# Three of four feed-forwards in a planned engine order, with seven-product pairs 5 to 21 and their sums in three PSUM banks

## The chip, the core and the metric

The kernel runs on one core of a Trainium2 chip. A core has a matrix engine (TensorE, PE in the profile), a vector engine (VectorE, DVE), an activation engine (ScalarE, ACT), a general engine (GpSimd, POOL) and one that issues transfers (SyncE, SP). Matrix products land in PSUM, which has eight banks of 128 partitions by 512 f32 values. All other tiles lie in SBUF. Each engine runs its own instructions strictly in order, and waits at an instruction until the semaphores it names are set. The metric is the device time of one execution in microseconds (us).

## The reference, cut to what matters

```python
D_MODEL, SEQ, D_FF, DEPTH = 1024, 512, 2816, 2

def swiglu_ffn(x, w_gate, w_up, w_down):
    return (jax.nn.silu(x @ w_gate) * (x @ w_up)) @ w_down

for layer in range(DEPTH):
    h = h + 0.5 * swiglu_ffn(rms_norm(h, ffn1_norm[layer]), ffn1 weights[layer])
    # layer 0: Conformer convolution module; layer 1: stick-breaking attention on shared K and V
    h = h + mixer(rms_norm(h, mix_norm[layer]))
    h = h + 0.5 * swiglu_ffn(rms_norm(h, ffn2_norm[layer]), ffn2 weights[layer])
    # after layer 0: K and V for layer 1 = rms_norm(h, kv_norm) @ w_kv
return rms_norm(h, final_norm)
```

All values are f32. There are four feed-forwards, numbered 0 to 3 here in the order of execution. Numbers 1 and 2 follow each other without a mixer between them (the end of layer 0 and the start of layer 1).

## The kernel before, in words

**Tiles.** Activations lie with features on partitions and the 512 tokens along the free axis, in eight chunks of 128 features. Every f32 operand of a product is split into a high part (a cast to fp32r, on ScalarE, line L249) and a low part (the difference, on VectorE, L250), and a product is three matmuls: high by high, high by low, low by high (`mm3`, L397 to L399). A weight unit is 128 x 1024 f32 (512 KB). It is loaded by SyncE into one of three `raw` buffers and split into one of three `whi` and one of three `wlo` buffers (`fetch`, L364 to L387). `unit` (L389) hands out the oldest unit and loads the next one.

**A feed-forward** (`ffn`, L490 to L640) works in three thirds, hidden columns 0 to 7, 8 to 15 and 16 to 21 of 128 each. In a third, each hidden column f takes a gate unit and an up unit, its *pair*. Then eight down products `pd` (L397 to L399) add the third to the residual `xpar` (L631). A **plain pair** is 2 units x 8 chunks x 3 = 48 matmuls with 512 columns. A **seven-product pair** (`seven`, L532 to L576) computes the same two products as a 2 x 2 block product by the Strassen-Winograd scheme: seven block products of 4 x 3 matmuls with 256 columns, 84 in all. Its weight sums are made by `sevens` (L327 to L362) from the two raw units: `st` holds two sums (L344, L346), L345 and one more subtraction make two others in place in `raw`, and all are split like weights (`sh`/`sl`, `uh`/`ul`, second unit `whi`/`wlo`). These buffers exist once each. The matching sums of the activations are made once per feed-forward by `right_sums` (L501 to L519). The list `SEVEN` names the columns that are computed so: 11, 10 and 11 of the 22 in feed-forwards 1, 2 and 3, mixed with plain pairs. Feed-forward 0 has none.

**The sums of the seven products.** A seven-product pair takes three PSUM banks `pg`. ScalarE copies the first product (`m1`, L560) and the third (`m5`, L564) out, VectorE makes `v6` (L562) and `v7` (L566) and adds the rest in L568 to L576.

**Norm.** Each feed-forward's input is normalised by a factor per token. `Norm.chunk` (L457 to L478) takes each residual chunk when it is final: ScalarE writes `xhi_f` (L463) and its square `sq_f` (L476), VectorE writes `xlo_f` (L464) and adds the square to `acc_f` (L477). When all eight are in, `factor` (L480) sums `acc_f` over features with four small matmuls (`token_sums`, L425 to L430), takes the root, and spreads it to `rb`, which multiplies the gate and up products where they leave PSUM (L571, L572, L576; L611 in plain pairs).

**Order.** The program is written feed-forward by feed-forward as above, and the framework's scheduler orders the instructions of each engine across these statements, by its own estimate of when each is ready. PSUM banks of a feed-forward rotate through one tag with seven buffers.

The program's three feed-forwards with seven-product pairs run, in the profiled execution, from about 553 to 905 us (number 1), 905 to 1260 us (number 2) and 1537 to 1885 us (number 3).

Of the kernel before, what the change touches and what calls it, by code (L numbers as in the profile page):

```python
# [198 lines left out]
def decoder_kernel(ctx, tc, xin, gu, dna, dnb, pw1, pw2, kq, wv, wo, out):  # L199
# [126 lines left out]

    def sevens(i, src):  # L327

        p = beside_hidden[0]
        raw = [wp.tile([P, UNIT], F32, name=f"raw{i}_{o}", tag="raw", bufs=3) for o in range(2)]
        hi, lo = (
            [wp.tile([P, UNIT], F32R, name=f"{n}{i}_0", tag=n, bufs=3),
             p.tile([P, UNIT], F32R, name=f"{n}{i}_1", tag=n, bufs=1)]
            for n in ("whi", "wlo")
        )
        for o in range(2):
            nc.sync.dma_start(raw[o], src[o])
        st = p.tile([P, UNIT], F32, name=f"st{i}", tag="st", bufs=STS)  # L340
        a11, a12, a21, a22 = (quarter(raw[o], e) for o in range(2) for e in range(2))
        s1, s2 = (quarter(st, e) for e in range(2))
        split(hi[0], lo[0], raw[0])
        V.tensor_add(s1, a21, a22)  # L344
        V.tensor_sub(a21, a11, a21)  # L345
        V.tensor_sub(s2, s1, a11)  # L346
        sh, sl = (p.tile([P, UNIT], F32R, name=f"s{n}{i}", tag=f"s{n}", bufs=1) for n in "hl")
        split(sh, sl, st)
        split(hi[1], lo[1], raw[1])
        V.tensor_sub(a12, a12, s2)  # L350
        uh, ul = (p.tile([P, NC // 2, P], F32R, name=f"u{n}{i}", tag=f"u{n}", bufs=1) for n in "hl")
        split(uh, ul, a12)

        def part(h, l, e):
            return lambda q: (quarter(h, e)[:, q, :], quarter(l, e)[:, q, :])

        return {
            "11": part(hi[0], lo[0], 0), "12": part(hi[0], lo[0], 1),
            "s3": part(hi[1], lo[1], 0), "22": part(hi[1], lo[1], 1),
            "s1": part(sh, sl, 0), "s2": part(sh, sl, 1),  # L360
            "s4": lambda q: (uh[:, q, :], ul[:, q, :]),
        }  # L362
# [127 lines left out]
    def ffn(idx, norm, done, early=None, beside=None, sums=None, late=None, tail=None):  # L490
        with ExitStack() as c:
# [6 lines left out]
            halves = [slice(0, T // 2), slice(T // 2, T)]
            right = []

            def right_sums(q):  # L501


                x = []
                for k in (2 * q, 2 * q + 1):
                    f = tp.tile([P, T], F32, name=f"xs{idx}_{k}", tag="sq", bufs=2)
                    V.tensor_add(f, *(y.bitcast(F32) for y in norm.x[k]))
                    x.append(f)
                b11, b12, b21, b22 = (y[:, h] for y in x for h in halves)
                t = hp.tile([P, 2 * T], F32, name=f"ts{idx}_{q}", tag="st", bufs=STS)  # L510
                t1, t2, t3, t4 = (t[:, j * T // 2 : (j + 1) * T // 2] for j in range(4))
                V.tensor_sub(t1, b12, b11)
                V.tensor_sub(t2, b22, t1)
                V.tensor_sub(t3, b22, b12)
                V.tensor_sub(t4, b21, t2)
                tiles = [sums_at(q, o) for o in range(2)]
                for o, (h, l) in enumerate(tiles):
                    split(h, l, t[:, o * T : (o + 1) * T])
                right.append(tiles)  # L519

            def sums_at(q, o):
                if sums is not None:
                    return [
                        sums[0].tile([P, T], F32R, name=f"t{n}{idx}_{q}_{o}", tag=sums[1] + n, bufs=NC)
                        for n in ("hi", "lo")
                    ]
                return [
                    hp.tile([P, T], F32R, name=f"t{n}{idx}_{q}_{o}", tag=f"t{n}", bufs=NC)
                    for n in ("hi", "lo")
                ]  # L530

            def seven(n, tg, tu):  # L532
                w = unit()

                def x(row, h):
                    return lambda q: [y[:, halves[h]] for y in norm.x[2 * q + row]]

                def t(j):
                    return lambda q: [y[:, halves[j % 2]] for y in right[q][j // 2]]


                at_ = [
                    ps.tile([P, T], F32, name=f"pg{n}_{j}", tag="ps", bufs=7)[:, : T // 2]
                    for j in range(3)
                ]
                m1, m5, v6, v7 = (
                    hp.tile([P, T // 2], F32, name=f"{m}_{n}", tag=m, bufs=1)
                    for m in ("m1", "m5", "v6", "v7")
                )

                def product(j, left, rhs, first):
                    for q in range(NC // 2):
                        a, b, d = w[left](q), rhs(q), at_[j]
                        last_ = q == NC // 2 - 1
                        PE.matmul(d, a[0], b[0], start=first and q == 0, stop=False, skip_group_check=True)  # L555
                        PE.matmul(d, a[0], b[1], start=False, stop=False, skip_group_check=True)  # L556
                        PE.matmul(d, a[1], b[0], start=False, stop=last_, skip_group_check=True)  # L557

                product(0, "11", x(0, 0), True)
                A.copy(m1, at_[0])  # L560
                product(1, "s2", t(1), True)
                V.tensor_add(v6, at_[1], m1)  # L562
                product(2, "s1", t(0), True)
                A.copy(m5, at_[2])  # L564
                product(1, "s3", t(2), False)
                V.tensor_add(v7, at_[1], m1)  # L566
                product(2, "s4", x(1, 1), False)
                V.tensor_add(tg[:, halves[1]], at_[2], v6)  # L568
                product(0, "12", x(1, 0), False)
                product(1, "22", t(3), False)  # L570
                V.tensor_mul(tg[:, halves[1]], tg[:, halves[1]], rb[:, halves[1]])  # L571
                V.tensor_mul(tg[:, halves[0]], at_[0], rb[:, halves[0]])  # L572
                last[0] = A.activation(tg, tg, AF.Silu)
                V.tensor_add(tu[:, halves[1]], v7, m5)
                V.tensor_add(tu[:, halves[0]], at_[1], m1)
                V.tensor_mul(tu, tu, rb)  # L576
# [903 lines left out]
```

## Time and profile before

| | |
|---|---|
| median of 3 runs | 1906.84 us (1905.96 to 1907.18) |
| span of the profiled execution | 1904.9 us |
| TensorE busy | 1884.1 us, 99% of the span |
| VectorE busy | 1318.5 us, 69% |
| ScalarE busy | 872.7 us, 46% |
| seven-product pairs | 32 of 66 pairs in feed-forwards 1 to 3 |

In the lines of the profile, `L398 PE MATMUL pg<-xlo_f,whi` is line 398 of the kernel before, on TensorE, writing tile `pg` from `xlo_f` and `whi`. A timeline row begins with the start in us and the duration in us. A bracket at its end tells how long the engine was idle ahead of it and what ended that. The rows of windows give a stretch of the span, its length, and for each engine its busy time with the number of instructions in brackets; then come the granted TensorE clock (1.00 is full speed), the share of time in which DMA engines were busy, and GB/s. The time of a matmul in a record holds its passage through the array, which overlaps the next one, so that the cost of a matmul in a dense stretch is the distance between starts.

### The profile page before, as it was taken

To read this page: it belongs to the slowest core of one execution; us is meant where nothing else is said; L and a number is where in the kernel's file an instruction comes from. 1 tells how busy PE (TensorE), PEld (TensorE's weight loads), DVE (VectorE), ACT (ScalarE), POOL (GpSimd) and SP (SyncE) were. 2 spreads that over 40 slices of the span, in tenths; PEclk is the share of its full clock that TensorE was granted. 3 is DMA by queue.
4 is the path that set the end of the run, shared out by engine and by line. 5 is a ranking of instruction groups with operands and counts; after the bars stand their busy time and mean duration, and the time that the engine had idled before them with its cause. 6 is when DMAs were issued, how large, how long until landed. Compare 5 with 4: busy or idle time off the path is not lost.

```text
span 1904.9 us, 26577 instructions
## 1 busy us (share of the span) xinstructions
PE 1884.1 (99%) x10236; PEld 1630.4 (86%) x10236; DVE 1318.5 (69%) x2139; ACT 872.7 (46%) x1385; POOL 288.1 (15%) x267
## 2 busy tenths in 40 slices
PE   9999999999999999999999999999999999999997
PEld 7888888878998889898888988888888788898896
DVE  6544434589869577576775857778989688676575
ACT  5423424586644234244333423446778644343333
POOL 0212302079700000000000000004554100000001
PEclk9999999999999999999999999999999999999998
DMA  5756746444422323333433232442323133332322
GB/s 203 251 180 232 275 146 216 158 172 144 161 78 89 105 89 117 100 94 96 143 111 100 89 111 89 127 155 83 89 70 93 49 123 100 100 95 95 111 86 70
DMA packets 74254, 237.84 MB, mean 125 GB/s; under 512 B 8464, under 2 KB 11152, under 8 KB 74128
## 3 DMA queue, kind: packets, MB, share of 16 engines
q1 hardware_dynamic: 65776, 209.41, 34.0%
q10 hardware_dynamic: 8352, 26.74, 3.8%
q8 instruction: 80, 1.31, 0.3%
q14 instruction: 46, 0.38, 0.1%
HBM read 200.46 MB, written 31.46 MB: 122 GB/s over the span
## 4 chain that ended last, share of the span: by engine, by line
PE 94%; DVE 2%; POOL 1%; ACT 1%; issue 1%; DMA 0%; POOLq 0%; DVEq 0%; ACTq 0%
PE pg L397 11%; PE pg L398 11%; PE pg L399 11%; PE pd L398 8%; PE pd L397 8%; PE pd L399 8%; PE pg L557 6%; PE pg L556 6%; PE pg L555 6%; PE z L1192 2%; PE pa L397 1%; PE pa L398 1%; PE pa L399 1%; PE pv L397 1%; PE pk L397 1%
## 5 line engine op out<-in xcount | busy, mean ns | idle before, releaser
L249 ACT CAST whi<-raw 128x1024 fp32r<-128x1024 f32 (+2 forms) x310 | 313.2, 1013 | 634.6 <-PE pd L398 226.8
L250 DVE TENSOR_TENSOR wlo<-raw,whi 128x1024 fp32r<-128x1024 f32 (+2 forms) x310 | 367.8, 1191 | 43.1 <-ACT whi L249 42.7
L398 PE MATMUL pg<-xlo_f,whi 128*128 128x512 f32 x896 | 349.7, 391 | 0.0
L397 PE MATMUL pg<-xhi_f,whi 128*128 128x512 f32 x896 | 349.0, 391 | 0.6 <-ACT whi L249 0.6
L399 PE MATMUL pg<-xhi_f,wlo 128*128 128x512 f32 x896 | 349.4, 390 | 0.0
L398 PE MATMUL pd<-hlo,whi 128*128 128x512 f32 x686 | 266.2, 389 | 0.0
L399 PE MATMUL pd<-hhi,wlo 128*128 128x512 f32 x686 | 265.1, 389 | 0.0
L397 PE MATMUL pd<-hhi,whi 128*128 128x512 f32 x686 | 264.1, 389 | 0.0
L397 PEld LDWEIGHTS pg<-xhi_f,whi 128*128 128x128 f32 x896 | 169.0, 189 | 35.2 <-ACT whi L249 1.5
L399 PEld LDWEIGHTS pg<-xhi_f,wlo 128*128 128x128 f32 x896 | 168.6, 188 | 34.7 <-DVE wlo L250 0.3
L398 PEld LDWEIGHTS pg<-xlo_f,whi 128*128 128x128 f32 x896 | 168.8, 188 | 33.6
L631 DVE SCALAR_TENSOR_TENSOR xpar<-pd,xpar 128x512 f32<-128x512 f32 x93 | 63.7, 689 | 170.6 <-PE pd L399 170.6
L399 PEld LDWEIGHTS pd<-hhi,wlo 128*128 128x128 f32 x686 | 128.8, 188 | 26.8
L397 PEld LDWEIGHTS pd<-hhi,whi 128*128 128x128 f32 x686 | 128.8, 188 | 26.7
L398 PEld LDWEIGHTS pd<-hlo,whi 128*128 128x128 f32 x686 | 128.8, 188 | 26.6
L1092 POOL TENSOR_SCALAR_AFFINE_SELECT tri<-ones 128x128 f32<-128x128 f32 x1 | 0.6, 592 | 703.7 <-DVE tu L612 703.7
L250 POOL TENSOR_TENSOR plo<-praw,phi 128x1024 fp32r<-128x1024 f32 x24 | 59.0, 2461 | 275.7 <-ACT phi L249 273.9
L875 POOL TENSOR_TENSOR ws<-ws,pr 128x256 f32<-128x256 f32 (+1 forms) x90 | 91.0, 1023 | 58.2 <-ACT pr L873 54.6
L249 ACT CAST hhi<-tu 128x512 fp32r<-128x512 f32 x88 | 54.3, 621 | 87.9 <-DVE tu L586 49.2
L886 DVE SCALAR_TENSOR_TENSOR pc<-gl,xpar,pc 128x512 f32<-128x512 f32 (+1 forms) x145 | 88.3, 646 | 3.9 <-PE pc L865 2.2
L611 DVE TENSOR_TENSOR tu<-pg,r_f 128x512 f32<-128x512 f32 x56 | 38.6, 689 | 74.2 <-PE pg L399 74.2
L556 PE MATMUL pg<-tlo,whi 128*128 128x256 f32 x256 | 72.5, 283 | 0.0
(359 smaller groups left out, 4195.0 us busy)
## 6 DMA issues: line engine op xcount, KB each, us to landing
raw<-in_gu_dram SPq DMA_DIRECT2D x174, 512.0 KB, 3.5
raw<-in_dna_dram SPq DMA_DIRECT2D x64, 512.0 KB, 3.6
praw<-in_pw_dram SPq DMA_DIRECT2D x24, 512.0 KB, 4.4
aparth<-phi ACTq DMA_DIRECT2D x24, 512.0 KB, 2.7
apartl<-plo ACTq DMA_DIRECT2D x24, 512.0 KB, 3.8
raw<-in_dnb_dram SPq DMA_DIRECT2D x32, 384.0 KB, 3.4
whi<-aparth SPq DMA_DIRECT2D x21, 512.0 KB, 3.3
wlo<-apartl SPq DMA_DIRECT2D x21, 512.0 KB, 4.2
```

What stands on the lines that cost most here:

```text
L249: ins = A.copy(dst_hi, src)
L250: (G if on_pool else V).tensor_sub(dst_lo, src, dst_hi.bitcast(F32))
L397: PE.matmul(ps, w[0], x[0], start=first, stop=False)
L398: PE.matmul(ps, w[0], x[1], start=False, stop=False)
L399: PE.matmul(ps, w[1], x[0], start=False, stop=last)
L555: PE.matmul(d, a[0], b[0], start=first and q == 0, stop=False, skip_group_check=True)
L556: PE.matmul(d, a[0], b[1], start=False, stop=False, skip_group_check=True)
L557: PE.matmul(d, a[1], b[0], start=False, stop=last_, skip_group_check=True)
L611: V.tensor_mul(tu, pt[1], rb)
L631: V.scalar_tensor_tensor(res[d], pd, 0.5, res[d], op0=ALU.mult, op1=ALU.add)
L875: add("G", 1.28 * f + 0.1 * half, lambda pr=pr: G.tensor_add(accp, accp, pr()[:, at0]), r=[pr], w=[at_], rank=rank)
L886: add("V", 0.66 * f + 0.06 * half, lambda x=x, q=q: V.scalar_tensor_tensor(pc(), x(), q, pc(), op0=ALU.mult, op1=ALU.add), r=[gl], w=[pc], ...
```

## The change

Feed-forward 0 stays in `ffn`. Feed-forwards 1, 2 and 3 move to a new function `planned`, which lists every step with its engine, an assumed duration, what it reads and writes, and a rank, in a `Plan`. The plan then picks, again and again, the step that can start earliest by the assumed durations (among equals the lowest rank), and the instructions of TensorE, VectorE and ScalarE are issued exactly in that order, without the framework's scheduler.

```diff
-SEVEN = {1: (5, 6, 8, 9, 11, 12, 14, 16, 17, 19, 20), 2: (6, 8, 10, 11, 13, 14, 16, 17, 19, 20), 3: (5, 6, 8, 9, 11, 12, 14, 16, 17, 19, 20)}
+SEVEN = {i: tuple(range(5, 22)) for i in (1, 2, 3)}
...
-    ffn(1, n_f2, n_f1.chunk, sums=(xp, "x"))
+    planned(1, n_f2, n_f1, sums=(xp, "x"), ahead=2)
...
-        ffn(2, n_f1, n_mix.chunk, early=kv_input, sums=(kvp, ""), late=kv_back)
+        planned(2, n_f1, n_mix, early=kv_input, sums=(kvp, ""), late=kv_back)
...
-    ffn(3, n_f2, n_out.chunk, tail=tail)
+    planned(3, n_f2, n_out, tail=tail, ahead=TAIL)
```

In `planned`, three of the eight PSUM banks are set apart for the sums of seven-product pairs (`u0`, `u1`, `g1`), and five are left to rotate. The sums are no longer added up by VectorE: after a product, ScalarE copies the bank's content to the bank where the next products go on adding.

```diff
+            banks = [ps.tile([P, T], F32, name=f"bank{idx}_{i}", tag="ps", bufs=8) for i in range(8)]
+            seeds = {x: banks[i][:, :N2] for i, x in enumerate(("u0", "u1", "g1"))}
...
+            add("PE", 0.5, lambda: token_sums(ss()[:, :4], norm.acc), w=[ss], rank=-2)
...
+                for x in seeds.values():
+                    PE.matmul(x, onesr, norm.x[0][0][:, :N2], start=True, stop=True)
+            add("PE", 0.4, seed, w=list(seeds), rank=-2)
...
+                product(g0b, g0, w["11"], x(0, 0), [], True, r_)
+                add("A", 0.35, lambda: A.copy(ub, g0b()), r=[g0], w=[u], rank=rank - 1)
+                product(mb, m, w["s1"], t(0), sums_, True, r_)
+                product(lambda: ub, u, w["s2"], t(1), sums_, False, r_)
+                add("A", 0.35, lambda: A.copy(m5(), mb()), r=[m], w=[m5], rank=rank - 0.5)
+                add("A", 0.35, lambda: A.copy(gb, ub), r=[u], w=[g1], rank=rank - 1)
+                product(g0b, g0, w["12"], x(1, 0), [], False, r_)
+                add("V", 0.35, lambda: V.tensor_mul(tg()[:, lo_], g0b(), rb[:, lo_]), r=[g0, "rb"], w=[tg], rank=rank)
+                product(lambda: ub, u, w["s3"], t(2), sums_, False, r_)
+                add("A", 0.35, lambda: A.copy(u3(), ub), r=[u], w=[u3], rank=rank - 1)
...
+                product(lambda: gb, g1, w["s4"], x(1, 1), [], False, r_)
...
+                product(lambda: ub, u, w["22"], t(3), sums_, False, r_)
```

The assumed durations are 3.0 us for a weight transfer, 0.95 and 1.14 for the two halves of a split, 1.44 for a product of twelve matmuls, 0.682 for three matmuls with 512 columns, and 0.15 from the end of a step to the start of one that waits for it. Weights of a seven-product pair are loaded by `load_seven`: the same operations as `sevens`, with the second unit's transfer issued first, and the same number of buffers (`raw` 3, the rest of the sums one each). `kv_input` and `kv_back`, which put the K and V input away and fetch it back in feed-forward 2, become steps of the plan. Counted over the program, TensorE has 693 matmul rows more.

The order listings that follow give line, operation, tiles and shape; `bank1_7` is the eighth PSUM bank in feed-forward 1, and numbers behind names only keep tiles apart.

**TensorE at the start of feed-forward 2.** Before, `ss`, the token sums of the normalisation (they read `acc_f1_1`, complete when the last chunk of the residual is final), stand behind 30 matmuls of the first pair (`pg2_0_0`, `pg2_0_1`); the last of them are:

```order
L399 MATMUL pg2_0_1_8288<-xhi_f1_1_1_8029,wlo147_8170 128x512
L398 MATMUL pg2_0_0_8287<-xlo_f1_1_7_8228,whi146_8136 128x512
L399 MATMUL pg2_0_0_8287<-xhi_f1_1_7_8227,wlo146_8137 128x512
L429 MATMUL ss_f1_1_8249<-onesD_74,acc_f1_1_5081 128x1 x4
L397 MATMUL pg2_0_1_8288<-xhi_f1_1_2_8062,whi147_8169 128x512
```

In the changed kernel the same sums (here in `bank2_3`, L387) follow directly on the last down product of feed-forward 1:

```order
L355 MATMUL bank1_7_5095<-hhi1_21_8253,whi139_8398 128x512
L356 MATMUL bank1_7_5095<-hlo1_21_8258,whi139_8398 128x512
L357 MATMUL bank1_7_5095<-hhi1_21_8253,wlo139_8405 128x512
L387 MATMUL bank2_3_8511<-onesD_74,acc_f1_1_5081 128x1 x4
L637 MATMUL bank2_0_8508<-xhi_f1_1_0_8277,onesr_72 128x256
L355 MATMUL bank2_4_8512<-xhi_f1_1_0_8277,whi140_8428 128x512
L356 MATMUL bank2_4_8512<-xlo_f1_1_0_8285,whi140_8428 128x512
```

The token sums moved from behind 30 matmuls that do not need the last squares to the head of the stage. The first of the three seed matmuls (L637) is shown; the first pair comes behind them. Feed-forwards 1 and 3 start the same way.

**VectorE in the second third of feed-forward 1.** Before, pair 9's sums (`v6`, `v7`, `tg1_9`, `tu1_9`) stand between the weight sums of the seven-product pair that is loaded next (`st115`, `sl115`):

```order
L562 TENSOR_TENSOR v6_1_9_6335<-pg1_9_1_6331,m1_1_9_6333 128x256
L344 TENSOR_TENSOR st115_6313<-raw115_1_6306 128x4x128
L250 TENSOR_TENSOR hlo1_8_6300<-tu1_8_6189,hhi1_8_6299 128x512
L345 TENSOR_TENSOR raw115_1_6306<-raw115_0_6305,raw115_1_6306 128x4x128
L346 TENSOR_TENSOR st115_6313<-st115_6313,raw115_0_6305 128x4x128
L250 TENSOR_TENSOR sl115_6320<-st115_6313,sh115_6319 128x1024
L566 TENSOR_TENSOR v7_1_9_6336<-pg1_9_1_6331,m1_1_9_6333 128x256
L568 TENSOR_TENSOR tg1_9_6303<-pg1_9_2_6332,v6_1_9_6335 128x256
```

In the changed kernel every pair of this third is a seven-product pair. While pair 12 is computed (`tg1_12`, `tu1_12`; its weights are `114`), the weights of pair 13 (`115`) are made:

```order
L570 TENSOR_TENSOR st115_6716<-st115_6716,raw115_0_6754 128x4x128
L573 TENSOR_TENSOR raw115_1_6641<-raw115_0_6754,raw115_1_6641 128x4x128
L506 TENSOR_TENSOR wlo115_0_6805<-raw115_0_6754,whi115_0_6788 128x1024
L506 TENSOR_TENSOR sl115_6809<-st115_6716,sh115_6803 128x1024
L731 TENSOR_TENSOR tu1_12_6823<-u3_1_12_6807,m5_1_12_6750 128x256
L734 TENSOR_TENSOR tg1_12_6783<-bank1_2_5090,m5_1_12_6750 128x256
L732 TENSOR_TENSOR tu1_12_6823<-tu1_12_6823,r_f2_0_5096 128x256
L735 TENSOR_TENSOR tg1_12_6783<-tg1_12_6783,r_f2_0_5096 128x256
L738 TENSOR_TENSOR tu1_12_6823<-bank1_1_5089,r_f2_0_5096 128x256
L506 TENSOR_TENSOR wlo115_1_6844<-raw115_1_6641,whi115_1_6838 128x1024
```

Every pair of the second and the last third now has such a block, eight pairs and six pairs in a row. The `raw` buffer that the last of these rows (`wlo115_1`) reads for the last time is the one into which the first unit of the next pair (`raw116_0`) is loaded; for some other pairs it is the one that `ul` (L577) reads last.

**ScalarE at the same place.** Before, its copies took two sums out of PSUM into SBUF (`m1`, `m5`):

```order
L249 CAST whi112_1_6108<-raw112_1_6106 128x1024
L560 COPY m1_1_9_6333<-pg1_9_0_6330 128x256
L564 COPY m5_1_9_6334<-pg1_9_2_6332 128x256
L249 CAST hhi1_8_6299<-tu1_8_6189 128x512
L249 CAST sh115_6319<-st115_6313 128x1024
```

Now copies from bank to bank stand in the queue behind casts of weights, and TensorE's next product on that bank waits for the copy:

```order
L730 COPY u3_1_11_6678<-bank1_0_5088 128x256
L698 ACTIVATE tg1_11_6662<-tg1_11_6662 128x512
L505 CAST whi114_1_6714<-raw114_1_6496 128x1024
L505 CAST uh114_6731<-raw114_0_6595 128x512
L722 COPY bank1_1_5089<-bank1_4_5092 128x256
L505 CAST hhi1_11_6736<-tu1_11_6682 128x512
L725 COPY m5_1_12_6750<-bank1_6_5094 128x256
```

What moved is who waits: `L722` fills the bank in which pair 12's product with `s2` goes on, and it comes behind the `tg1_11` activation and two casts of weights 114, which are pair 12's own.

More of the change, by code (lines that the diff above doesn't have):

```diff
@@ L319, in opened @@
         return src, raw, hi, lo
-    beside_hidden = [None]
     def quarter(t, e):
         return t.rearrange("p (q e c) -> p q e c", e=2, c=P)[:, :, e, :]
[L327 to L362, printed above, removed]
     def fetch():
@@ L488, in factor, with ffn @@
             return spread(ps, small, self.name, r, tag=tags[1], bufs=bufs)
-    def ffn(idx, norm, done, early=None, beside=None, sums=None, late=None, tail=None):
+    def ffn(idx, norm, done, early=None, beside=None):
         with ExitStack() as c:
@@ L495, in ffn @@
             ps = pool(c, f"ps{idx}", space=PSUM)
-            beside_hidden[0] = hp
             rb = norm.factor(ps) if idx else None
[L498 to L576, printed above, removed]
@@ L623, in ffn @@
                             beside(pp_)
-                if third == 2 and late is not None:
-                    late()
-                for d in range(NC - TAIL if tail is not None and third == 2 else NC):
+                for d in range(NC):
                     w = unit()
@@ L1059, in decoder_kernel, with kv_input, kv_back @@
         kvd = spill.tile([P, NC * T], F32, name="kvd")
-        def kv_input(third, r):
-            if third:
-                return
+        def kv_input(plan, r):
             for c in range(NC):
-                t = tp.tile([P, T], F32, name=f"kvt{c}", tag="sq", bufs=2)
-                V.scalar_tensor_tensor(t, res[c], col("kv", c), r, op0=ALU.mult, op1=ALU.mult)
-                nc.sync.dma_start(kvd[:, c * T : (c + 1) * T], t)
-        def kv_back():
-            for c in range(NC):
-                t = tp.tile([P, T], F32, name=f"kvb{c}", tag="sq", bufs=2)
-                nc.sync.dma_start(t, kvd[:, c * T : (c + 1) * T])
-                hi = kvp.tile([P, T], F32R, name=f"kvh{c}", tag="hi", bufs=NC)
-                lo = kvp.tile([P, T], F32R, name=f"kvl{c}", tag="lo", bufs=NC)
-                split(hi, lo, t)
+                t = Buf("sq", lambda c=c: tp.tile([P, T], F32, name=f"kvt{c}", tag="sq", bufs=2))
+                plan.add("V", 0.66, lambda t=t, c=c: V.scalar_tensor_tensor(
+                    t(), res[c], col("kv", c), r, op0=ALU.mult, op1=ALU.mult), r=["rb", ("res", c)], w=[t], rank=6.5)
+                plan.add("D", 2.0, lambda t=t, c=c: nc.sync.dma_start(kvd[:, c * T : (c + 1) * T], t()),
+                         r=[t], w=["kvd"], rank=6.5)
+        def kv_back(plan, rank):
+            for c in range(NC):
+                t = Buf("sq", lambda c=c: tp.tile([P, T], F32, name=f"kvb{c}", tag="sq", bufs=2))
+                plan.add("D2", 2.5, lambda t=t, c=c: nc.sync.dma_start(t(), kvd[:, c * T : (c + 1) * T]),
+                         r=["kvd", "sums"], w=[t], rank=rank)
+                hi = Buf("-", lambda c=c: kvp.tile([P, T], F32R, name=f"kvh{c}", tag="hi", bufs=NC))
+                lo = Buf("-", lambda c=c: kvp.tile([P, T], F32R, name=f"kvl{c}", tag="lo", bufs=NC))
+                split_steps(plan, hi, lo, t, 0.55, 0.6, rank)
                 kvx.append((hi, lo))
         n_mix = Norm("mix_1", "mix_1")
-        ffn(2, n_f1, n_mix.chunk, early=kv_input, sums=(kvp, ""), late=kv_back)
+        planned(2, n_f1, n_mix, early=kv_input, sums=(kvp, ""), late=kv_back)
+        kvx = [(hi(), lo()) for hi, lo in kvx]
         away = spill.tile([P, NC * T], F32, name="away")
```

267 lines of the change are left out of this document (248 added, 19 removed).

## The prediction

> **What bounds the kernel now.** I read the busy shares first, then the chain of work that ended last, then the windows of the three feed-forwards that the change touches.
>
> ```profile
> PE 1884.1 (99%) x10236; PEld 1630.4 (86%) x10236; DVE 1318.5 (69%) x2139; ACT 872.7 (46%) x1385; POOL 288.1 (15%) x267
> PE 94%; DVE 2%; POOL 1%; ACT 1%; issue 1%; DMA 0%; POOLq 0%; DVEq 0%; ACTq 0%
> 558.00:908.00 350.00, 350.00 (x1982) 308.55 (x1982) 246.17 (x380) 133.53 (x181) 0.00 (x0) 1.00 0.31 99
> 908.00:1260.00 352.00, 351.12 (x1950) 307.59 (x1949) 249.72 (x391) 137.32 (x186) 3.03 (x7) 1.00 0.36 116
> 1540.00:1885.00 345.00, 345.00 (x1991) 305.74 (x1991) 236.87 (x371) 126.44 (x171) 0.00 (x0) 1.00 0.29 94
> ```
>
> TensorE is busy 99% and carries 94% of the last chain. In the three stretches it is busy 350.00 of 350.00, 351.12 of 352.00 and 345.00 of 345.00 us at a granted clock of 1.00. VectorE is at about 70% there and ScalarE below 40%. So in these stages every matmul less is time less, as long as nothing makes TensorE wait, and every wait that the change puts on TensorE is time more. All work of VectorE and ScalarE is covered now, and the prediction is about whether it still will be.
>
> **1. Fewer matmul cycles: a gain.** The cost of a matmul is the distance between starts in a dense stretch.
>
> ```profile
> 574.02:603.26 29.24, 29.24 (x130) 24.21 (x129) 27.95 (x48) 14.06 (x21) 0.00 (x0) 1.00 0.29 90
> 574.02 0.39 PE L398 MATMUL pg<-xlo_f,whi 128*128 128x512 f32 x1
> 603.26 0.39 PE L398 MATMUL pg<-xlo_f,whi 128*128 128x512 f32 x1
> 689.79:698.19 8.40, 8.40 (x73) 8.40 (x71) 5.97 (x11) 3.61 (x5) 0.00 (x0) 1.00 0.41 122
> 689.79 0.28 PE L557 MATMUL pg<-thi,wlo 128*128 128x256 f32 x1
> 698.07 0.28 PE L557 MATMUL pg<-thi,sl 128*128 128x256 f32 x1
> ```
>
> From 574.02 to 603.26 there are 129 distances, all of 512 columns: 29.24 / 129 = 0.2267 us. From 689.79 to 698.07 there are 69 distances of 256 columns (the window counts also what reaches over its edges): 8.28 / 69 = 0.1200 us. A plain pair is 48 x 0.2267 = 10.88 us, a seven-product pair 84 x 0.1200 = 10.08, so one conversion gains 0.80 us. Converted are 17 - 11, 17 - 10 and 17 - 11 pairs, 19 in all: **-15.2 us**. The two prices are for matmuls that follow each other without a wait, and the 0.1200 is already that of seven-product pairs in a row.
>
> **2. The token sums at the head of a stage: a loss.** The rows are the start of feed-forward 2 (TensorE, VectorE, ScalarE), then those of feed-forwards 1 and 3.
>
> ```profile
> 905.16 0.39 PE L399 MATMUL pd<-hhi,wlo 128*128 128x512 f32 x1
> 905.39 0.39 PE L397 MATMUL pg<-xhi_f,whi 128*128 128x512 f32 x1
> 912.19 0.95 PE L429 MATMUL ss_f<-onesD,acc_f 128*128 128x1 f32 x8
> 905.59 0.69 DVE L631 SCALAR_TENSOR_TENSOR xpar<-pd,xpar 128x512 f32<-128x512 f32 x1 [0.73 <-PE pd L399]
> 907.59 0.75 DVE L464 SCALAR_TENSOR_TENSOR xlo_f<-xpar,xhi_f 128x512 fp32r<-128x512 f32 x1
> 908.25 0.68 DVE L477 TENSOR_TENSOR acc_f<-acc_f,sq_f 128x512 f32<-128x512 f32 x1
> 906.32 0.72 ACT L463 ACTIVATE xhi_f<-xpar 128x512 fp32r<-128x512 f32 x1
> 906.94 0.62 ACT L476 ACTIVATE sq_f<-xpar 128x512 f32<-128x512 f32 x1
> 553.26 0.40 PE L397 MATMUL pg<-xhi_f,whi 128*128 128x512 f32 x1
> 556.23 0.69 DVE L477 TENSOR_TENSOR acc_f<-acc_f,sq_f 128x512 f32<-128x512 f32 x1
> 1537.34 0.39 PE L397 MATMUL pg<-xhi_f,whi 128*128 128x512 f32 x1
> 1540.21 0.68 DVE L477 TENSOR_TENSOR acc_f<-acc_f,sq_f 128x512 f32<-128x512 f32 x1
> ```
>
> Today the last down product is free at 905.39, the next pair starts at once, and the token sums come at 912.19, long after `acc_f` is done at 908.25 + 0.68 = 908.93. In the changed order the sums stand first on TensorE, and behind them wait the seeds and the whole first pair, which TensorE cannot reorder. The chain that it waits for is residual (905.59, 0.69), `xhi_f` (906.32, 0.72), `xlo_f`, `acc_f`. In the order before, a weight split delayed `xlo_f` from 907.04, when `xhi_f` ends, to 907.59; in the new order only a short sum stands there. So `acc_f` ends at 908.4 instead of 908.93, and TensorE idles from 905.39 to about 908.5: 3.1 us. For feed-forward 3 the same reading gives 1537.34 to 1540.4 (half a microsecond less than 1540.89): 3.1. Feed-forward 1 keeps its order ahead of the sums: 553.26 to 556.92, 3.7. Together 9.9 us. Nothing else stands ahead in TensorE's order to fill it. The nine seeds cost 9 x 0.12 = 1.1. **+11.0 us.** Bounds: if the planner's order lets ScalarE and VectorE run the shortest chain (0.69 + 0.72 or 0.62 in ACT's next turn + 0.69, with 0.1 to 0.2 between), each start costs 2.2, in all 6.6 + 1.1 = 7.7; at most it is today's full chain, 3.5 + 3.7 + 3.5 + 1.1 = 11.8.
>
> **3. Seven-product pairs in long rows: a wait that isn't there now.** Today plain pairs stand between seven-product pairs and the scheduler mixes their matmuls; 10.88 us of TensorE work that needs only two splits cover the sums of the next pair. Now eight pairs follow each other in the second third and six in the last one, each in 10.08 us. The prices on VectorE and of a transfer:
>
> ```profile
> 600.29 1.22 DVE L250 TENSOR_TENSOR wlo<-raw,whi 128x1024 fp32r<-128x1024 f32 x1
> 601.42 0.69 DVE L345 TENSOR_TENSOR raw<-raw,raw 128x512 f32<-128x512 f32 x1
> 602.02 0.68 DVE L346 TENSOR_TENSOR st<-st,raw 128x512 f32<-128x512 f32 x1
> 592.54 0.42 DVE L513 TENSOR_TENSOR ts<-xs,ts 128x256 f32<-128x256 f32 x1
> 592.88 0.69 DVE L507 TENSOR_TENSOR xs<-xhi_f,xlo_f 128x512 f32<-128x512 f32 x1
> 789.84 1.22 DVE L250 TENSOR_TENSOR wlo<-raw,whi 128x1024 fp32r<-128x1024 f32 x1 [0.17 <-ACT whi L249]
> 794.64 0.69 DVE L344 TENSOR_TENSOR st<-raw 128x512 f32<-128x512 f32 x1 [3.57 <-DMA raw<-in_gu_dram]
> 797.05 2.35 DVE L250 TENSOR_TENSOR wlo<-raw,whi 128x1024 fp32r<-128x1024 f32 x2
> 803.87 0.69 DVE L344 TENSOR_TENSOR st<-raw 128x512 f32<-128x512 f32 x1 [0.87 <-DMA raw<-in_gu_dram]
> ```
>
> By starts, VectorE takes 1.13 us for 128x1024, 0.60 for 128x512 and 0.34 for 128x256. A seven-product pair now gives it 3, 7 and 6 of these: 3.4 + 4.2 + 2.0 = 9.6 of 10.08 us. It has no room to catch up. A freed `raw` buffer is back in use after 3.58 us (789.84 + 1.22 = 791.06 to 794.64) at best, and after 4.47 (799.40 to 803.87) as the second of two transfers.
>
> The loop that sets the pace is: first raw unit landed, VectorE's block, buffer freed, transfer, next one landed. For weights 115 the ten rows of the order are 2 x 0.60, 3 x 1.13 and 5 x 0.34, 6.3 us; with the transfer and the waits of dependent neighbours 10.0. Where the buffer is freed by a later row it is longer. Worked out row by row, the five loops from weights 112 to 117 take 10.3, 11.6, 12.1, 10.0 and 11.4 us, against 10.08 for a pair. The third pair's unit lands 3.6 us into the second pair, at 13.9 after the row's start. It must land 2.5 to 2.9 before its pair (two sums and a split, 0.60 + 0.60 + 1.13, and a pick-up of 0.2). So the slack of pairs three to eight is 3.8, 3.0, 1.8, 0.2, -0.1 and -1.1 us.
>
> When that slack is used up, the waits of TensorE's products are those on ScalarE, whose copies stand in order behind casts of weights.
>
> ```profile
> L249 ACT CAST whi<-raw 128x1024 fp32r<-128x1024 f32 x266 | 279.6, 1052 | 569.2 <-PE pd L398 198.7 <-PE pg L398 181.8 <-PE pg L556 69.5
> L560 ACT COPY m<-pg 128x256 f32<-128x256 f32 x32 | 11.8, 370 | 21.2 <-PE pg L557 20.9
> L573 ACT ACTIVATE tg<-tg 128x512 f32<-128x512 f32 x32 | 20.1, 629 | 11.7 <-DVE tg L571 11.7
> ```
>
> A copy (0.37 us) that finds a late cast (1.05) or the activation (0.63) ahead of it is late by up to their length, and the product behind it with it; in time it has the 1.44 us of the product between (12 x 0.1200), and costs nothing. Walked through by hand, the eight pairs lose 0.25, 0.95, 0.3 and 1.0 us, 2.5 in all, the six pairs the first two, 1.2, and the first third (pairs 5 to 7) nothing. That is 3.7 per feed-forward, **+11.1 us** for three. Bounds: with 0.3 us less per loop only the last pair is late, 1 us a feed-forward, 3; with all transfers at 4.47, each of the five loops is 0.9 longer, which makes the last pairs 3 to 4 us later, 22 in all. I take the walk, since it rests on the shorter trip, the commoner one.
>
> **4. Edits at no cost.** The bank copies replace two adds of VectorE and add one copy of 0.37 us; they are counted in 3. `kv_input` and `kv_back` keep their operations, 8 transfers each way, beside feed-forward 2, where VectorE has 100 us of idle time; if a third of a pair were late behind them it would cost 1 us. Five rotating banks for seven: a plain pair takes two, down products one each, and VectorE empties one 0.2 + 0.69 after its end, against 24 x 0.2267 = 5.4 us for the next, so nothing.
>
> **Sum**: -15.2 + 11.0 + 11.1 = +6.9. On the profiled span, 1904.9 + 6.9 = 1911.8; the median is 1.9 us above that span, so the median comes to 1906.84 + 6.9 = 1913.7, and I say 1913.5.
>
> **The clock: a rule and a row.** Elsewhere in this trace TensorE did go without dense work, at the end and at the start.
>
> ```profile
> 1891.27 0.39 PE L1351 MATMUL pb_out0a<-dg_out,onesr 128*128 128x256 f32 x2
> 1893.00:1894.00 1.00, 0.10 (x1) 0.01 (x1) 0.93 (x4) 0.18 (x1) 1.00 (x3) 1.00 0.69 236
> 1894.00:1895.00 1.00, 0.00 (x0) 0.00 (x0) 0.97 (x2) 0.00 (x0) 1.00 (x2) 0.54 0.69 238
> 1.26 4.45 PE L651 MATMUL pw<-wz 128*128 128x512 bf16 x10 [1.26 <-DVE wz L648]
> ```
>
> The granted clock is still 1.00 up to 1894.00 and then falls to half, about 2.5 us behind the last full matmuls (1891.27 + 0.39). At half clock a 512-column matmul takes 4.45 / 10 = 0.445 us, twice 0.2267. The idle stretches of part 2 are longer than 2.5 us, so they may lose the clock as well. The Trainium skill, page "TensorE: Matmul & The Clock Gate", section "What's actually happening", says that the clock is halved after an idle window of about 3.4 us and given back after about as long a busy one, and that the window runs freely. By that a start that loses it would cost about 1.7 us beside its idle time, an estimate from that page, and a start of 3.1 us would rarely lose it; no run here shows one of this length.
>
> **The rivals.**
> - *The clock falls at the starts.* The mechanism: TensorE idles 3.1 to 3.7 us, the clock falls at 2.5 as at 1894, and the first matmuls run at 0.445 for some us. At the kernel's start 4.45 us of matmuls all ran at half rate, so I take 4 to 8 us at half rate for each start, which costs 2 to 4 us, 6 to 12 in all: about 1922. For: the 2.5 us. Against: small matmuls at 1892 to 1894 blur when idleness began. The clock-gate page is the rule beside it. Chance 0.15.
> - *The loading loop is worse.* Transfers come as the second of two, 4.47 us, since the two units of a pair are issued one behind the other: 22 instead of 11.1, about 1925, and up to 1930 with the clock. Chance 0.12.
> - *The rows nearly keep up.* The loops are 0.3 us shorter, and only the starts cost: -15.2 + 11.0 + 0 to 4, 1902.6 to 1906.6, so about 1905. For: VectorE has 0.5 us spare per pair and the planner put every block in the order of its own earliest starts. Chance 0.18.
> - *The other side: the chain at the starts is short.* Place: the last chunk's squares. If they go ahead of its high part, or the records' waits are shorter under the new order, a start costs 2.2 us, and with rows that keep up the sum is -15.2 + 7.7 = -7.5: 1899.3. It decides below 3.3 us per transfer and 2.5 per start. For: TensorE's gain is certain. Against: the order puts `xhi_f` first. Chance 0.13.
> - That the pairs aren't converted is ruled out by the order, where TensorE has 693 more rows: 19 x 36 and the nine seeds.
>
> **How the numbers follow.** My forecast (1904 to 1918, by the bounds of part 3 around 3 and 16) has 0.42. A measurement of this kernel tells about 0.2%, 3.8 us, from no change: 1903.0 and 1910.7. The other side is faster: 0.13. The rows that nearly keep up, and the low part of my forecast (0.12), are no change: 0.30. The rest of the forecast (0.30), the clock and the worse loop are slower: 0.57. The range reaches from 1901, which leaves out most of the short-chain case, to 1930, which takes in the clock and the worse loop.
>
> **What would show it.** In the profile after, at the three starts TensorE should be idle about 3 us, released by VectorE's `acc_f`; the windows there show whether the clock falls. From the fifth pair of a row on, TensorE should wait for ScalarE's bank copies or for VectorE's `sl` and `wlo`, and VectorE for `raw` transfers; the distance of pairs should be 10.08 up to there. No idle at the starts would make part 2 wrong; dense rows of pairs, part 3; a distance unlike 10.08 without waits, part 1.

## The result, and the profile after

The changed kernel takes 1916.84 us (median of 4 runs, 1915.85 to 1917.69) against 1906.84 before. The ratio is 1.0052, with a 95% interval of 1.0038 to 1.0067: 10.0 us slower (7.2 to 12.8). The forecast was 1913.5.

The busy times on the page of the changed kernel, then the windows of its three feed-forwards, with the same columns as before:

```profile
PE 1880.7 (98%) x10929; PEld 1659.5 (87%) x10929; DVE 1382.6 (72%) x2265; ACT 947.3 (49%) x1563; POOL 281.5 (15%) x267
```

The windows:

```profile
552.00:911.00 359.00, 352.25 (x2212) 319.85 (x2210) 265.02 (x419) 158.35 (x240) 0.00 (x0) 0.99 0.29 97
911.00:1267.50 356.50, 351.46 (x2210) 319.93 (x2210) 276.56 (x437) 164.11 (x248) 4.44 (x7) 0.99 0.34 115
1545.50:1897.00 351.50, 347.24 (x2231) 317.46 (x2229) 259.34 (x412) 152.34 (x232) 0.00 (x0) 1.00 0.28 93
```

TensorE is no longer busy throughout: 6.75, 5.04 and 4.26 us of these stretches are idle, and in two of them the mean granted clock is 0.99. The waits of TensorE in the changed kernel, in us in total, number of times, and the longest:

```profile
PE bank L387 <- DVE acc_f L435: 6.6, 2, 3.5
...
PE bank L387 <- DVE acc_f L774: 3.7, 1, 3.7
PE bank L684 <- ACT u L730: 3.5, 7, 1.1
PE bank L686 <- DVE sl L506: 1.4, 3, 0.5
...
PE bank L684 <- ACT bank L726: 0.6, 1, 0.6
...
PE bank L684 <- ACT bank L722: 0.2, 1, 0.2
```

The first two rows are the token sums at the head of the three stages, 10.3 us. The others are waits in the rows of seven-product pairs, 5.7 us. Around the longest of them:

```profile
738.71 0.28 PE L686 MATMUL bank<-xhi_f,ul 128*128 128x256 f32 x1
740.05 0.39 PE L684 MATMUL bank<-thi,whi 128*128 128x256 f32 x1 [1.06 <-ACT u L730]
740.27 0.28 PE L685 MATMUL bank<-tlo,whi 128*128 128x256 f32 x1
```

The distances of starts are 1.34 and 0.22 us instead of 0.12 twice, so the idle 1.06 us cost 1.32. Summed over all neighbouring matmuls of 256 columns in the three stages, the seeds left out, the distances exceed 0.12 us by 9.5 us in this kernel. *By distances* below means this sum.

The clock is in windows around the starts: for each stage the stretch of waiting, then the matmuls behind it.

```profile
552.00:556.00 4.00, 0.46 (x5) 0.25 (x3) 3.71 (x6) 2.19 (x3) 0.00 (x0) 1.00 0.13 25
556.00:563.00 7.00, 7.00 (x24) 5.84 (x24) 6.28 (x29) 1.24 (x2) 0.00 (x0) 0.53 0.16 62
911.00:915.00 4.00, 0.32 (x3) 0.32 (x3) 3.77 (x7) 2.13 (x3) 0.00 (x0) 0.97 0.17 71
915.00:921.50 6.50, 6.50 (x21) 5.53 (x22) 4.79 (x20) 0.62 (x1) 0.00 (x0) 0.50 0.02 4
1545.50:1549.00 3.50, 0.48 (x4) 0.14 (x2) 2.86 (x5) 2.19 (x3) 0.00 (x0) 1.00 0.00 0
1549.00:1553.00 4.00, 4.00 (x17) 3.52 (x18) 2.97 (x16) 0.00 (x0) 0.00 (x0) 0.58 0.00 0
```

TensorE counts as fully busy in the second row of each pair, and yet does only half its work: the clock had fallen at all three starts. The time lost is the missing share of the clock: 7.00 x 0.47 + 6.50 x 0.50 + 4.00 x 0.42 = 8.2 us. Another 0.3 lies just outside these three windows.

One such matmul and one at full clock in the first stage:

```profile
558.23 0.63 PE L356 MATMUL bank<-xlo_f,whi 128*128 128x512 f32 x1
558.65 0.63 PE L357 MATMUL bank<-xhi_f,wlo 128*128 128x512 f32 x1
...
563.52 0.39 PE L357 MATMUL bank<-xhi_f,wlo 128*128 128x512 f32 x1
563.75 0.40 PE L355 MATMUL bank<-xhi_f,whi 128*128 128x512 f32 x1
```

The starts are 0.42 us apart at first and 0.23 later. An average share of busy time does not show this loss; the distance of starts and the clock column do.

### The profile page after: what moved, and what is told of

It reads as the page before. It is cut to its first block, busy times and chain, and to the rows that moved or that the text cites. A ratio compares the mean times of both kernels' runs of the same rounds, so it can differ in the third digit from the quotient of the medians.

```text
span 1915.9 us, 28166 instructions
## 1 busy us (share of the span) xinstructions
PE 1880.7 (98%) x10929; PEld 1659.5 (87%) x10929; DVE 1382.6 (72%) x2265; ACT 947.3 (49%) x1563; POOL 281.5 (15%) x267
## 5 line engine op out<-in xcount | busy, mean ns | idle before, releaser
L355 PE MATMUL bank<-hhi,whi 128*128 128x512 f32 x510 | 198.5, 389 | 0.0
L356 PE MATMUL bank<-hlo,whi 128*128 128x512 f32 x510 | 198.5, 389 | 0.0
L357 PE MATMUL bank<-hhi,wlo 128*128 128x512 f32 x510 | 198.4, 389 | 0.0
L250 DVE TENSOR_TENSOR wlo<-raw,whi 128x1024 fp32r<-128x1024 f32 (+3 forms) x109 | 128.9, 1186 | 24.9 <-ACT whi L249 24.7
L357 PE MATMUL pg<-xhi_f,wlo 128*128 128x512 f32 x352 | 137.0, 390 | 0.4 <-DVE wlo L250 0.4
L356 PE MATMUL pg<-xlo_f,whi 128*128 128x512 f32 x352 | 136.9, 389 | 0.0
L355 PE MATMUL pg<-xhi_f,whi 128*128 128x512 f32 x352 | 136.5, 391 | 0.3 <-ACT whi L249 0.3
L506 DVE TENSOR_TENSOR wlo<-raw,whi 128x1024 fp32r<-128x1024 f32 x102 | 124.4, 1220 | 4.4 <-ACT whi L505 4.4
L684 PE MATMUL bank<-thi,whi 128*128 128x256 f32 x408 | 116.5, 286 | 4.3 <-ACT u L730 3.5
L686 PE MATMUL bank<-thi,sl 128*128 128x256 f32 x408 | 115.7, 284 | 1.4 <-DVE sl L506 1.4
```

The source lines that it names most:

```text
L250: (G if on_pool else V).tensor_sub(dst_lo, src, dst_hi.bitcast(F32))
L355: PE.matmul(ps, w[0], x[0], start=first, stop=False)
L356: PE.matmul(ps, w[0], x[1], start=False, stop=False)
L357: PE.matmul(ps, w[1], x[0], start=False, stop=last)
L506: plan.add("V", v, lambda: V.tensor_sub(lo(), src(), hi().bitcast(F32)), r=[src, hi, *r], w=[lo, *w], rank=rank)
L684: PE.matmul(d, a[0], b[0], start=start and q == 0, stop=False, skip_group_check=True)
```

## The experiments

All ratios are to runs of the kernel before on the same chip, whose medians there were 1906.84 to 1907.23 us.

**Late token sums.** A step that does nothing tells the plan that `acc_f` comes 5 us into the stage, so that the first pair's matmuls stand ahead of the token sums.

```diff
-            add("PE", 0.5, lambda: token_sums(ss()[:, :4], norm.acc), w=[ss], rank=-2)
+            add("-", 5.0, lambda: None, w=["acc0"], rank=-9)
+            add("PE", 0.5, lambda: token_sums(ss()[:, :4], norm.acc), r=["acc0"], w=[ss], rank=-2)
```

> The token sums are given a start 5 us into the stage, so that TensorE begins each of the three feed-forwards with the first pair's matmuls. Theory: the three starts cost 10.2 us of idle time and 8.4 us of matmuls at half clock (6.4, 6.9 and 3.5 us at a granted clock of 0.5, of which half is lost). Both go: 1916.8 - 18.6 = about 1898, the granted clock stays 1.00 at the starts, and the waits in the rows of seven-product pairs stay about 5.7 us. Rival 1, the halved clock is only what the records show of an idle engine and costs nothing: only the idle time goes, about 1906.6. Rival 2, the factor that comes 5 us later delays the first pairs' outputs and the wait moves there: 1912 or more.

Measured: 1905.68 us, ratio 0.9995 (0.9987 to 1.0004), 10.9 us less than the changed kernel by the ratios. Windows of this run at the first start:

```profile
553.00:557.00 4.00, 2.54 (x12) 2.15 (x13) 3.70 (x7) 1.93 (x3) 0.00 (x0) 1.00 0.22 59
557.00:565.00 8.00, 8.00 (x41) 6.73 (x40) 7.48 (x26) 2.44 (x4) 0.00 (x0) 1.00 0.10 39
```

The clock stays at 1.00. The gain lies between the theory's 18.6 and the rival's 10.2, and its waits tell part of what was given back:

```profile
PE bank L632 <- DVE dg_f L629: 2.1, 2, 1.7
PE bank L638 <- ACT xhi_f L421: 1.6, 1, 1.6
```

The factor's matmul (`dg_f`) now waits, since its root starts later and TensorE is not slowed any more. The seeds wait in feed-forward 1 for the high part of chunk 0. Both are rival 2 in small, 3.7 us. From the last matmul ahead of each stage to the last of the stage itself, this profile is 14.8 us shorter than the changed kernel's over the three stages, near 18.6 - 3.7 = 14.9. That the medians differ by less comes from the profiled executions: this one (1904.02) was the fastest of its eleven, that of the changed kernel (1917.69) the slowest of its four.

**Filling the wait.** 28 matmuls stand ahead of the token sums, which stay at the head of the stage.

```diff
+            def fill():
+                x0 = norm.x[norm.order[0]][0]
+                for _ in range(28):
+                    PE.matmul(seeds["u0"], onesr, x0[:, :N2], start=True, stop=True)
+            add("PE", 3.4, fill, w=["u0"], rank=-3)
             add("PE", 0.5, lambda: token_sums(ss()[:, :4], norm.acc), w=[ss], rank=-2)
```

> The token sums stay at the head of the stage, but 28 matmuls of 256 columns (28 x 0.12 = 3.4 us) into a bank that is seeded afterwards are put ahead of them: the end of the wait stays where it is, but TensorE isn't idle. Theory: the granted clock stays 1.00 and the 8.4 us at half clock go: about 1908.4. Rival, the clock has no part in it: 1916.8, or up to 1917.5 where the filler outlasts the wait.

Measured: 1915.07, ratio 1.0042 (1.0028 to 1.0055), only 1.9 us less by the ratios. Windows of the first start:

```profile
551.50:556.50 5.00, 5.00 (x45) 5.00 (x44) 4.60 (x7) 3.41 (x5) 0.00 (x0) 1.00 0.01 2
556.50:563.00 6.50, 6.22 (x36) 5.24 (x35) 6.12 (x21) 1.25 (x2) 0.00 (x0) 1.00 0.26 83
```

Two rows of TensorE's waits in the same run:

```profile
PE bank L636 <- DVE dg_f L633: 2.9, 2, 1.6
PE bank L357 <- DVE wlo L548: 0.9, 1, 0.9
```

The clock stays at 1.00, as the theory said, but the time did not follow by 8.4. Two things were in the way. At full clock TensorE reaches the factor's matmul sooner and waits there, 3.8 us in the two rows: part of the loss at half clock had covered a wait that was due anyway. And the filler with the rest of the wait is 0.6 us longer than the idle time was. Added up over the stages, this profile is 4.4 us shorter, with 6.4 us less idle time and 10.1 us of filler. So the clock itself accounts for 4.4 - 6.4 + 10.1 = 8.1 us, near the 8.2 from the windows. By the medians less of it is left; the difference to the profile lies within what executions of one kernel differ outside these stages.

**The list of before in the planned order.**

```diff
-SEVEN = {i: tuple(range(5, 22)) for i in (1, 2, 3)}
+SEVEN = {1: (5, 6, 8, 9, 11, 12, 14, 16, 17, 19, 20), 2: (6, 8, 10, 11, 13, 14, 16, 17, 19, 20), 3: (5, 6, 8, 9, 11, 12, 14, 16, 17, 19, 20)}
```

> The planned order and the bank copies stay, but SEVEN is the list of before (32 pairs instead of 51, none in long rows). Theory: the 19 conversions are lost again (+15.2 us) and the 5.7 us of waits in the rows go: 1916.8 + 15.2 - 5.7 = about 1926.3. Rival 1, a conversion gains nothing once VectorE is loaded to 95% in the rows: 1911 to 1917. Rival 2, the waits come from the bank copies and not from the rows: about 1932.

Measured: 1925.03, ratio 1.0097 (1.0083 to 1.0110). That is the theory within 1.3 us. No wait for a bank copy is left in this run, so the bank copies alone cost TensorE nothing, and the waits belong to the rows of pairs.

**The planner's prices.** First both, then each alone: 3.6 for 3.0 us of a weight transfer, and 1.05 for 0.95 of a cast.

```diff
-                add("D", 3.0, lambda: nc.sync.dma_start(full[0]()[:, :n], src), w=[full[0]], rank=rank)
+                add("D", 3.6, lambda: nc.sync.dma_start(full[0]()[:, :n], src), w=[full[0]], rank=rank)
...
-                split_steps(plan, hi[0], lo[0], raw[0], 0.95, 1.14, rank)
+                split_steps(plan, hi[0], lo[0], raw[0], 1.05, 1.14, rank)
```

> Only the planner's assumed durations change: 3.6 us for a weight transfer in place of 3.0, 1.05 for a cast of 128x1024 in place of 0.95. Theory: the waits in the rows come from an order that was made for a shorter loading loop, with the copy u3 behind a cast of 1.05: with true prices they halve, about 1914, and the starts stay as they are. Rival: the loop itself is too long and no order mends it: 1916.8 or more, with waits of 5 us or more in the rows.

> Only the planner's price of a weight transfer changes, 3.6 for 3.0. Theory: this price alone makes the order in which u3 comes ahead of the cast sh and each raw buffer is freed in time, so that it comes to the 1912.5 of both prices, with waits of 1 us or less in the rows. Rival, the cast's price does it: 1916.8 and waits of 5 us or more.

> Only the planner's price of a cast of 128x1024 changes, 1.05 for 0.95. Theory (the transfer's price decides): about 1916, the waits in the rows stay above 4 us. Rival: 1912.5, waits below 1 us.

Measured: both prices 1912.50 (ratio 1.0030, 1.0018 to 1.0041), the transfer's alone 1913.06 (1.0032, 1.0019 to 1.0044), the cast's alone 1917.28 (1.0055, 1.0043 to 1.0068). The transfer's price decides. With it alone, one idle stretch of 0.3 us is left in the rows, and by distances they lose 1.4 us instead of 9.5. The medians show less of this, 3.8 us by the ratios: in this run's profile the stretches outside the three stages are 2.2 us longer than in the changed kernel's. What the price changes is seen on ScalarE in the changed kernel, ahead of TensorE's longest wait there:

```profile
734.71 0.36 ACT L726 COPY bank<-bank 128x256 f32<-128x256 f32 x1 [1.07 <-PE bank L686]
737.73 1.05 ACT L505 CAST whi<-raw 128x1024 fp32r<-128x1024 f32 x1 [2.67 <-DMA raw<-in_gu_dram]
738.69 1.04 ACT L505 CAST sh<-st 128x1024 fp32r<-128x1024 f32 x1
739.63 0.36 ACT L730 COPY u<-bank 128x256 f32<-128x256 f32 x1
```

ScalarE stands still for 2.67 us at the head of its queue, at a cast whose raw unit has not landed. Behind it stand another cast and the copy `u3`, and TensorE's matmul at 740.05 (above) waits for that copy. That the plan put the casts there because it took the unit to have landed follows from its price, 3.0 against a trip of 3.58, and is not seen in the trace itself. With the transfer's price at 3.6, the copy of the same pair (pair 12 of feed-forward 1) stands ahead of the second cast:

```profile
735.80 1.05 ACT L505 CAST whi<-raw 128x1024 fp32r<-128x1024 f32 x1 [1.07 <-DMA raw<-in_gu_dram]
737.26 0.37 ACT L730 COPY u<-bank 128x256 f32<-128x256 f32 x1 [0.40 <-PE bank L686]
737.52 1.06 ACT L505 CAST sh<-st 128x1024 fp32r<-128x1024 f32 x1
```

The raw unit is also there sooner: the cast of `whi` starts 2.86 us behind the pair's copy `m5` (732.94) here and 4.46 us behind it (733.27) in the changed kernel. How much of the gain comes from either was not separated.

**A shorter idle stretch.** The filler with 10 matmuls in place of 28.

> As the run with 28 filler matmuls, but with 10 (1.2 us), so that TensorE idles about 2.5, 2.6 and 1.9 us at the three starts instead of 3.7, 3.8 and 3.1. Theory: the clock is lost by an idle stretch of about 3 us and kept through one of 2.5: granted clock 1.00, about 1914.5 as with 28 matmuls, since what is won at the clock is partly given back at the wait for dg_f. Rival, 2.5 us without dense work is already enough, as the end of the kernel suggested: 1916.8 and a clock of 0.5 behind the starts.

Measured: 1914.11, ratio 1.0036 (1.0024 to 1.0049). The time is the one expected, but not for the reason given. The three token sums in TensorE's timeline:

```profile
556.14 1.05 PE L387 MATMUL bank<-onesD,acc_f 128*128 128x1 f32 x8 [2.37 <-DVE acc_f L435]
910.51 1.84 PE L387 MATMUL bank<-onesD,acc_f 128*128 128x1 f32 x8 [2.50 <-DVE acc_f L779]
1546.47 1.02 PE L387 MATMUL bank<-onesD,acc_f 128*128 128x1 f32 x8 [1.85 <-DVE acc_f L435]
```

The windows behind them:

```profile
556.00:563.00 7.00, 6.86 (x36) 5.82 (x36) 6.52 (x30) 1.32 (x3) 0.00 (x0) 1.00 0.20 70
910.50:917.00 6.50, 6.49 (x21) 5.63 (x22) 5.52 (x21) 0.65 (x2) 0.00 (x0) 0.50 0.01 4
1546.50:1552.00 5.50, 5.50 (x23) 4.62 (x24) 5.02 (x20) 0.62 (x1) 0.00 (x0) 0.71 0.00 0
```

The clock was kept behind an idle stretch of 2.37 us and lost behind 2.50 and 1.85. Both theories assumed a length that decides; here the shortest of the three lost the clock and a longer one did not. The last section shows what the three starts differ in.

**All of it together.** Late token sums, both prices, seeds that read the first chunk to be final, and 4.0 us for the root.

```diff
-            add("V", 2.4, root, r=[ss], w=["root"], rank=-2)
+            add("V", 4.0, root, r=[ss], w=["root"], rank=-2)
...
-                    PE.matmul(x, onesr, norm.x[0][0][:, :N2], start=True, stop=True)
+                    PE.matmul(x, onesr, norm.x[norm.order[0]][0][:, :N2], start=True, stop=True)
```

> Late token sums and the true prices together, with two mends of what the first runs left at the starts: the seeds read the first chunk that is final instead of chunk 0 (the last one in feed-forward 1, 1.6 us of waiting), and the root of the factor is given 4.0 us instead of 2.4 (its matmul waited 1.7 us for dg_f). Theory: what is left against before is -15.2 for the conversions, +1.1 for the seeds and about 1 of waits in the rows: 1907 - 13 = about 1894, with a granted clock of 1.00 at all starts. Rival, the parts don't add since the planner gives the time back elsewhere: 1900 or more, as the sum of the two single gains less what the first runs gave back.

Measured: 1895.55, ratio 0.9940 (0.9926 to 0.9953). It beats both kernels: 11.4 us faster than before. Its windows of the three feed-forwards:

```profile
552.40:901.50 349.10, 348.36 (x2211) 317.38 (x2211) 265.07 (x419) 158.29 (x239) 0.00 (x0) 1.00 0.30 99
901.50:1250.50 349.00, 348.41 (x2211) 317.16 (x2210) 275.33 (x437) 164.68 (x249) 6.17 (x7) 1.00 0.35 117
1530.00:1876.00 346.00, 344.77 (x2232) 316.01 (x2231) 259.50 (x413) 153.95 (x233) 0.00 (x0) 1.00 0.29 95
```

At most 1.2 us of a stage are idle, with the same rows of eight and six pairs, the same buffers and the same work on VectorE.

**The same with the list of before.** It measures the conversion alone.

> The mended version with the list SEVEN of before: 32 converted pairs, with planned order, late token sums, true prices and bank copies. Theory: what remains against before is the seeds (+1.1) and the few waits; the 19 conversions are worth 0.80 us each: 1895.6 + 15.2 - 1 = about 1909.5. Rival, the planned order itself is better or worse than the framework's scheduler by some us: 1903 or less, or 1914 or more.

Measured: 1908.66, ratio 1.0011 (1.0003 to 1.0020). The 19 conversions are worth 1.0011 - 0.9940 = 0.0071 of 1907 us, 13.5 us. By distances the rows lose 2.6 us in the version before this one and 0.8 here, so 1.8 us of waits have already been taken off: 15.3 without them. The planned order by itself is as good as the scheduler's, but for about 2 us, of which 1.1 are the seeds.

**Too high a price.** The transfer at 4.4 us.

> The mended version with an assumed transfer of 4.4 us, the longer of the two trips read from the profile of before, in place of 3.6. Theory: 3.6 already gives an order without waits, a price above the true one only loads no earlier: 1895 to 1897. Rival, the longer trip is the one that counts in the rows: the last waits there (0.7 us of a shown 1.3) go, 1894.

Measured: 1912.84, ratio 1.0031 (1.0019 to 1.0043), 17 us slower than with 3.6. Neither theory held. Rows of TensorE in this run:

```profile
714.04 0.39 PE L687 MATMUL bank<-xhi_f,wlo 128*128 128x256 f32 x1 [0.21 <-DVE wlo L506]
...
724.95 0.39 PE L687 MATMUL bank<-xhi_f,wlo 128*128 128x256 f32 x1 [0.21 <-DVE wlo L506]
```

These two pairs are 10.91 us apart instead of 10.08: at the head of the pair TensorE waits for the `wlo` of its first unit, which VectorE's order now puts behind sums of the pair before, and 2 us later for `sl`. An order made for late transfers is late itself. By distances the rows lose 20.6 us here and 2.6 with 3.6, so the rows hold the whole difference.

## Why the forecast was right, and where it was not

The sign came out, and the median lies 3.3 us above the forecast. One term was missing from the sum.

| term | forecast | measured |
|---|---|---|
| conversions | -15.2 | -15.3 (-13.5 with the rows' last waits in it) |
| idle at three starts | 9.9 | 10.3 |
| seeds | 1.1 | 1.1 at full clock |
| rows of pairs | 11.1 | 9.5 |
| halved clock | 0 | 8.2 |
| sum | +6.9 | +13.9 with -15.2; +10.0 by the medians |

The 9.5 us of the rows are by distances. The idle time there is less (5.7), since a record of 0.28 us hides a wait's first 0.16 and the matmul behind a wait takes 0.10 more. The terms fit the stages, which are 13.3 us longer in the profiled execution. Its span is only 11.0 longer, since the stretches outside, whose source is the same, were 2.2 us shorter in it. So the three stages cost twice the forecast's 6.9, and that the median still lies in 1904 to 1918, which the forecast kept for a clock that does not fall, is in part luck.

*Part 1, the conversions,* held: 15.3 us for 19 is 0.80 us for each, by the last pair of runs.

*Part 2, the token sums,* held to 0.4 us in the sum, with the waits read off the profile of before. By start it was 3.7 against 3.5 measured (feed-forward 1), 3.1 against 3.7 (2) and 3.1 against 3.0 (3). Feed-forward 2 was longer because the planner put `acc_f` of the chunk before, 0.68 us at 911.14, ahead of the last residual on VectorE, which starts at 911.74, 0.87 us after the last down product instead of 0.20.

*The clock* was the step that failed. The forecast had the row at 1894 that speaks for it, and gave it the chance of a rival, 0.15, at 6 to 12 us; it came in all three starts at 8.2. The Trainium skill, page "TensorE: Matmul & The Clock Gate", section "What's actually happening", puts the fall at an idle window of about 3.4 us. By that section alone a 3.0 us stretch would not have lost the clock; here it did, and even one of 1.85 us did. The row of the kernel's end, which the forecast read as 2.5 us, was nearer, but no length decides. That its window runs freely, as the forecast quotes the Trainium skill, agrees with the switches in the trace, which keep to steps of 3.413 us; but a step need not be idle to cost the clock (last section).

*Part 3, the rows,* had the place (`u3` behind casts, late raw units) and most of the size, but not the cause. The forecast took the loading loop itself to be too long for 10.08 us. The runs showed that the loop fits: with another assumed transfer time, 3.6 for 3.0, the same loop with the same buffers loses 2.6 us by distances in all three stages of the best version. What cost time was the order made for a shorter transfer, in which ScalarE stood at a cast for data under way with TensorE's copy behind it. The trip of 3.58 us that the forecast quoted was the hint: it was used to lengthen the loop, and not to ask what a plan that reckons with 3.0 would do wrongly.

## What to carry to other kernels

Where an order is fixed by assumed durations, compare each with its row in a profile before anything else: 0.6 us on one transfer cost about 4 us here by the medians (8 in the rows, by distances), and a price too high by 0.8 cost 17. An instruction that waits for the last result of one stage must not stand first on the bottleneck engine of the next; work that does not need it goes ahead. After any wait that leaves TensorE idle for some 2 us, look at the granted clock behind it: here the three losses came to 8.2 us beside 10.3 us of waiting.

## What was not expected of the hardware

TensorE's clock fell at starts with 3.0 to 3.7 us of idle time, and in one run at 2.50 and 1.85 us, while 2.37 us kept it; so the length of the idle stretch alone does not decide.

The times of the switches tell more. In the changed kernel the clock falls at 556.39, 914.79, 1525.77 and 1549.67 us, and is back at 563.21, 921.61, 1529.19 and 1553.08. Any two of these lie a whole number of steps of 3.413 us apart, to 0.02 us: the first two falls, 358.40 us, are 105 steps. The switches in each of the other profiles lie on such a raster too. So in these profiles the clock changes only at the raster's marks, and it was half for two steps, two steps and one step behind the three starts. The rows are cut at the marks. First come the steps ahead of the three falls at starts; then, of the run with 10 filler matmuls, the two steps that share the idle stretch of 2.37 us, and the steps ahead of its two falls at starts.

```profile
552.97:556.39 3.42, 0.59 (x6) 0.59 (x6) 3.14 (x5) 1.39 (x3) 0.00 (x0) 1.00 0.24 63
911.37:914.79 3.42, 0.08 (x1) 0.11 (x1) 3.19 (x6) 1.76 (x3) 0.00 (x0) 1.00 0.10 40
1546.26:1549.67 3.41, 0.78 (x8) 0.81 (x8) 2.99 (x5) 1.62 (x3) 0.00 (x0) 1.00 0.00 0
...
552.08:555.50 3.42, 1.70 (x15) 1.49 (x13) 3.12 (x6) 2.19 (x3) 0.00 (x0) 1.00 0.01 2
555.50:558.91 3.41, 2.77 (x18) 2.52 (x19) 3.24 (x10) 0.62 (x1) 0.00 (x0) 1.00 0.46 154
907.07:910.48 3.41, 0.94 (x9) 0.74 (x8) 3.18 (x6) 1.87 (x3) 0.00 (x0) 1.00 0.17 70
1545.36:1548.77 3.41, 2.30 (x16) 2.16 (x17) 3.17 (x11) 0.72 (x2) 0.00 (x0) 1.00 0.00 0
```

In the changed kernel the work in the three steps, 0.59, 0.08 and 0.78 us, is token sums alone, matmuls with one column. In the other run a mark at 555.50 cuts the stretch of 2.37 us in two, both steps keep 1.70 us of work or more, and the clock stays. Almost all of the 2.50 us lies in one step, which has 0.94 us of work, and the clock falls. The last row falls with 2.30 us of work, of which 0.89 are token sums, so that 1.41 are left. A step with 1.70 us of work without token sums kept the clock and one with 2.30 with them lost it, so the token sums did not count like other matmuls.

Counted without one-column matmuls over all twelve profiles, the clock fell behind every step at full rate with 1.59 us of work or less and behind one with 1.83, and stayed behind one with 1.70 (the row above) and behind all others, with 1.85 or more. That is about half of a step. This count was made after the runs, and no run was built to test it. The marks lie differently against the first instruction from profile to profile (one 0.02 us behind it in the changed kernel, one 2.19 us behind it in the best version), so that the same wait may cost the clock in one execution and not in another.

In the mixer ahead of feed-forward 3 the clock falls too, for one step in the changed kernel (1525.77) and for two in the best version (1507.47 to 1514.29), while it stays at 1.00 there in the profile of before. This is in none of the terms above. The scheduler's order in the mixer is not the same in the two kernels, so whether the order or the place of the marks did it is open.

Last, a half clock can hide a wait behind it: removing its loss of 8.1 us by fillers made the stages only 4.4 us shorter, and the medians about 2, until the wait for the factor was moved too.
